# Two sequences' gate projections as twelve jobs of seven block products between retention and merge, in an encoder layer on one core

## The chip, the cores and the metric

The kernel runs on one core of a Trainium2 chip. The metric is the time of one execution on the device in microseconds; the number given for a kernel is the median of several executions.

## What is computed

One encoder layer is applied with the same weights to two batches: a prompt of 512 tokens and a sample of 1024 tokens, all in fp32. Cut to what bears on the change, and then the final norm:

```python
u = rms_norm(x, norm1_g)
proj = u @ w_in                       # 1024 -> 5632
f, q, k, v, g_ret, g_a, g_b = jnp.split(proj, list(np.cumsum(IN_SPLITS[:-1])), axis=-1)
branch_a = fourier_mix(f) @ w_four_proj                     # 512 -> 1024
branch_b = bidirectional_retention(q, k, v, g_ret, ret_decay_logit) @ w_ret_proj
merged = jax.nn.sigmoid(g_a) * branch_a + jax.nn.sigmoid(g_b) * branch_b
x = x + merged @ w_out
u2 = rms_norm(x, norm2_g)
h_gate, h_val = jnp.split(u2 @ w_up, 2, axis=-1)
# a convolution of width 3 and a GELU on h_gate, times h_val, then w_down and the residual
```

`bidirectional_retention` normalises its output per head and multiplies it with `jax.nn.silu(g_ret)`. The three gates g_ret, g_a and g_b are 1024 columns each.

## The kernel before, in words

**Layout.** Activations lie with the features on the partitions and the tokens along the free axis. The 1536 tokens are three blocks of 512 columns: t = 0 is the prompt, t = 1 and 2 are the two halves of the sample. A feature block is 128 rows, so 1024 features are eight blocks k. What does not fit on chip is spilled to DRAM in tiles of 128x512 (256 KB): `ma` for the Fourier branch, `sb` for the g_b gate, `og` for the retention output, each by feature block n and token block t.

**Products.** An fp32 product is made of three matmuls of a rounded type: every operand is split into a high part (a cast on ScalarE, ACT, L74) and the rest (a subtraction on VectorE, DVE, L75), and `mm3` (L110 to L112) adds high times high, high times low, low times high. A gate projection for one column block n and one token block t is therefore 8 x 3 = 24 matmuls of 512 columns. There are 3 gates x 8 blocks n x 3 blocks t = 72 of them.

**Stages.** Head: norms, the Fourier projection and the two DFTs. Then the stage called four projection here (a loop over n, L458 to L492): for each n a weight slab `wfour` (L461) is loaded, the Fourier branch `br` is computed in 258-column matmuls, and the three g_a gates of that n are projected, sent through a sigmoid (`gate`, L308 to L312), multiplied with `br` (L491) and stored as `ma` (L492). Then retention: four head pairs; `ret_main` projects q, k, v, hands each chunk of 128 tokens to a side generator, and projects the six g_ret gates of the pair as filling work; `ret_store` transposes the normalised output (L643), multiplies it with the gate (L644) and stores `og` (L645). `gb_main` projects the g_b gates: one column block in the DFT, four behind `ret_main` beside the last chunks, three around the start of the merge. Then the merge: `og` is loaded and split, multiplied with the slabs of `w_ret_proj` (`wslab`, L93), combined with `sb` and `ma` (loaded at L878 and L879), multiplied with `w_out`, added to x, and split. Then the up-projection and the down-projection.

**The up-projection's scheme.** For t = 1, 2 together, and by halves for t = 0, the up-projection is done as a 2x2 block product in seven block products in place of eight (`quad`). `w_ops` loads a raw weight block of 1 MB and forms four differences of it on DVE, splitting all; seven activation operands (A11, S1, S2, A12, S3, S4, A22, four row blocks each, high and low) lie on chip. One up job is 7 x 4 x 3 = 84 matmuls of 512 columns. `quads` runs jobs behind each other, with the elementwise work of a job one job late.

**What sets the order.** The program is written out in order, and each engine runs its own instructions in that order. SyncE (SP) issues the loads and nearly all stores in one queue of program order: a store that waits for its data holds up every load written behind it. Filling work is pulled one step at a time by generators. Buffers come from pools with a fixed number per tag.

Of the kernel before, what the change touches and what calls it, by code (L numbers as in the profile page):

```python
# [14 lines left out]
P = 128  # L15
# [9 lines left out]
SL_F, SL_GA, SL_GRET, SL_QKV, SL_GB = 0, 4, 12, 20, 36  # L25
SL_RP, SL_WO, SL_DL = 44, 52, 60
N_SLABS = 62
# [8 lines left out]
def emit(ctx, tc, x, wsl, wup, wdq, wd0, wfour, tab, cst, rcst, vec, out):  # L36
# [4 lines left out]
    uctx, wctx = ExitStack(), ExitStack()  # L41
    upool = uctx.enter_context(tc.tile_pool(name="u", bufs=24))
# [25 lines left out]
    x2_d = [[spill(f"xx{n}_{t}") for t in range(3)] for n in range(KD)]  # L68

    def utile(kind, dtype=F32R):  # L70
        return upool.tile([P, TC], dtype, name=kind, tag=kind)
# [5 lines left out]
    state = {"ww": (1152, 1032)}  # L77
# [5 lines left out]
    def wtiles():  # L83
        wpool = state["w"]
        wide, cols = state["ww"]
        r = wpool.tile([P, wide], F32, name="wr", tag="wr", bufs=2)
# [73 lines left out]
    state["w"] = wctx.enter_context(tc.tile_pool(name="w", bufs=4, reuse_waits="tile"))  # L160
    bctx = ExitStack()
    rc = bctx.enter_context(tc.tile_pool(name="rc", bufs=1, reuse_waits="tile"))
    state.update(wx=bctx.enter_context(tc.tile_pool(name="wx", bufs=1, reuse_waits="tile")), turn=-1)
# [10 lines left out]
    class Prep:  # L174
# [15 lines left out]
        def scale(self):  # L190
            k = len(u[self.t][0])
            xs = self.xs[k]
            g = vc[:, V_G1 + k:V_G1 + k + 1]
            h, l = utile("uh"), utile("ul")
# [12 lines left out]
        def rows(self):  # L207
            ps = rstd_rows(rcol[self.t])
            rrow[self.t] = rc.tile([P, TC], F32, name=f"rrow{self.t}")
# [98 lines left out]
    def gate(pool, tag, ps, t, bufs=None):  # L308
        sg = pool.tile([P, TC], F32, name="sg", tag=tag, bufs=bufs)
        nc.vector.tensor_tensor(sg, ps, rrow[t], op=ALU.mult)  # L310
# [3 lines left out]
    def gb_main(ns, pool, tag, bufs=None):  # L314
# [122 lines left out]

    z10 = channel_dft(1, 0)
# [7 lines left out]
    for q in preps:  # L446
        q.rows()
    z11 = channel_dft(1, 1)
    fill = gb_main(range(1), fp, "f2", 13)
# [7 lines left out]
    f2 = f2ctx.enter_context(tc.tile_pool(name="f2", bufs=2, side="right", reuse_waits="tile"))  # L457
    for n in range(KD):  # L458
# [55 lines left out]
    class Seq:  # L514
        def __init__(self, hp, si):
            self.hp, self.si = hp, si
            self.S, self.qd, self.os = {}, {}, {}
            self.st = None
# [82 lines left out]
    def ret_states(sq):  # L601
# [10 lines left out]
        for q in range(nt):  # L612
# [24 lines left out]
            yield  # L637

    def ret_store(sq, q, i, sg):
# [4 lines left out]
        nc.vector.tensor_tensor(sg, ps, sg, op=ALU.mult)  # L644
        nc.sync.dma_start(og_d[2 * sq.hp + i][t], sg)  # L645

    def ret_stores(todo):
        for args in todo:
            ret_store(*args)
            yield  # L650

    def ret_main():
        for hp in range(4):
# [18 lines left out]
            wg = [wslab(SL_GRET + 2 * hp + i) for i in range(2)]  # L672
            todo = []
            for t in range(3):
                for i in range(2):
                    ps = bank()
                    for _ in proj_steps(ps, wg[i], u[t]):
                        yield
                    g = rp.tile([P, TC], F32, name="g", tag="g")
                    sg = rp.tile([P, TC], F32, name="sg", tag="sg", bufs=4)  # L680
                    nc.vector.tensor_tensor(g, ps, rrow[t], op=ALU.mult)
                    nc.scalar.activation(sg, g, AF.Sigmoid)
                    nc.gpsimd.tensor_tensor(sg, g, sg, op=ALU.mult)
                    todo.append((seqs[0], 0, i, sg) if t == 0 else (seqs[1], t - 1, i, sg))
                    yield
                if t == 0 and hp < 3:
                    decay_t(hp + 1)
                if t == 0:
                    sides.append(ret_stores(todo))
                    todo = []  # L690
            sides.append(ret_stores(todo))

    decay_t(0)
    drive(ret_main())
    drive(gb_main(range(1, 5), rp, "g"))
# [4 lines left out]
    cp = cctx.enter_context(tc.tile_pool(name="mrg", bufs=5, side="right", reuse_waits="tile"))  # L700

    def og_split(t):
        gh, gl = [], []
        for k in range(KD):
            o = cp.tile([P, TC], F32, name="og", tag="st")
            l = cp.tile([P, TC], F32R, name="gl", tag="gl", bufs=KD)
            h = cp.tile([P, TC], F32R, name="gh", tag="gh", bufs=KD)
# [6 lines left out]
    drive(gb_main(range(5, 6), cp, "st"))  # L714
    order = (1, 2, 0)
    og = og_split(order[0])
    drive(gb_main(range(6, 8), cp, "st"))
    bctx.close()
    wctx.close()
    uctx.close()  # L720


    def left(name, bufs=1, stack=ctx):
        return stack.enter_context(tc.tile_pool(name=name, bufs=bufs, reuse_waits="tile"))

    def right(name, bufs, stack):
        return stack.enter_context(tc.tile_pool(name=name, bufs=bufs, side="right", reuse_waits="tile"))
# [5 lines left out]
    state["ww"] = 2048, 1024  # L733
    obctx, occtx = ExitStack(), ExitStack()
# [3 lines left out]
    xp = left("xs", 6, nctx)  # L738
# [45 lines left out]

    def chain(*gens):
        for g in gens:
            yield from g
            yield

    def w_ops(src, w):  # L790
        raw = wp.tile([P, 2048], F32, name="wr", tag="wr", bufs=2)[:, :4 * w]
        nc.sync.dma_start(raw, src)
        b = raw.rearrange("p (b c) -> p b c", b=4)

        def hl(src, n):
            tag, bufs = ("w", 4) if n == 2 else ("w4", 1)
            l = wp.tile([P, n * 512], F32R, name=tag + "l", tag=tag + "l", bufs=bufs)[:, :n * w]
            h = wp.tile([P, n * 512], F32R, name=tag + "h", tag=tag + "h", bufs=bufs)[:, :n * w]
            split(h, l, src)
            return [(h[:, i * w:(i + 1) * w], l[:, i * w:(i + 1) * w]) for i in range(n)]  # L800

        b11, b21 = hl(raw[:, :2 * w], 2)
        ta = wp.tile([P, 1024], F32, name="wt", tag="wt", bufs=2)[:, :2 * w]
        nc.vector.tensor_tensor(ta.rearrange("p (b c) -> p b c", b=2), b[:, 2:4], b[:, 0:3:2], op=ALU.subtract)
        t1, t3 = hl(ta, 2)
        tb = wp.tile([P, 1024], F32, name="wt", tag="wt", bufs=2)[:, :2 * w]
        nc.vector.tensor_tensor(tb[:, :w], b[:, 3], ta[:, :w], op=ALU.subtract)
        nc.vector.tensor_tensor(tb[:, w:], b[:, 1], tb[:, :w], op=ALU.subtract)
        t2, t4 = hl(tb, 2)
        b22, = hl(b[:, 3], 1)  # L810
        return {"A11": b11, "A12": b21, "S4": b22, "A22": t4, "S1": t1, "S2": t2, "S3": t3}

    def product(ps, w, act, name, start=False):
        n = len(act[name])
        for k, (h, l) in enumerate(act[name]):
            c = slice(k * P, (k + 1) * P)
            wh, wl = w[name]
            mm3(ps, wh[:, c], wl[:, c], h, l, start and k == 0, k == n - 1, not start)

    def quad(w, act, cols, sink):  # L820

        a = bank(cols)
        product(a, w, act, "A11", start=True)
        sink("P1", a)
        yield
        c = bank(cols)
        product(c, w, act, "S1", start=True)
        product(a, w, act, "S2")
        sink("P1+P6", a)
        b = bank(cols)  # L830
        product(b, w, act, "A12", start=True)
        sink("P2", b)
        product(a, w, act, "S3")
        sink("P1+P6+P7,P5", (a, c))
        yield
        product(c, w, act, "S4")
        sink("P5+P3", c)
        product(a, w, act, "A22")
        sink("P1+P6+P7+P4", a)
        yield  # L840

    late = []

    def tick():
        for it in list(late):
            if next(it, late) is late:
                late.remove(it)

# [476 lines left out]
```

## Time and profile before

| | |
|---|---|
| median of 3 runs | 2282.09 us (2281.72 to 2283.24) |
| the profiled execution | 2279.94 us, span 2277.8 us, granted clock 0.991 |
| TensorE (PE) matmuls busy | 2228.0 us, 98% |
| DVE busy | 1474.6 us, 65% |
| ACT busy | 848.5 us, 37% |
| GpSimd (POOL) busy | 345.8 us, 15% |
| DMA moved | 273.30 MB, mean 120 GB/s |

The stages in the trace: head up to about 165 us, four projection 165 to 340, retention 340 to about 830, the g_b tail to 971, merge from 975, then the up- and down-projection. A busy PE row means that a matmul was in flight; a PE clock of 1.00 in a window means that the throttle granted full speed in all of it.

### The profile page before, as it was taken

How to read it: one execution, taken by the hardware profiler on the slowest of the kernel's cores; microseconds unless marked ns; L12 is line 12 of the kernel's file. 1: busy time of each engine (PE TensorE's matmuls, PEld its weight loads, DVE VectorE, ACT ScalarE, POOL GpSimd, SP SyncE). 2: the span in 40 equal slices, each digit the busy share in tenths (PEclk: the TensorE clock that was granted, in tenths of full speed). 3: DMA queues.
4: the chain of work that ended last, by engine and by line, in shares of the span. 5: the costliest groups of instructions: out<-in, count | busy, mean ns of one | idle time of the engine just before them, and what ended most of it. 6: DMA issues, size and time to landing. Idle time of an engine off the chain costs nothing. (4 is left out here: it accounts for less than half of the span.)

```text
span 2277.8 us, 29367 instructions
## 1 busy us (share of the span) xinstructions
PE 2228.0 (98%) x11294; PEld 1866.6 (82%) x11294; DVE 1474.6 (65%) x2555; ACT 848.5 (37%) x1373; POOL 345.8 (15%) x184
## 2 busy tenths in 40 slices
PE   8899999999999999999999999999989999999997
PEld 6788888888888888878887788888867878999986
DVE  7453434656556462255678886767689888999744
ACT  6251222223121221133334444434453446666413
POOL 2799601111212120010120000000000000000001
PEclk9999999999999999999999999999999999999999
DMA  5252220111102012276756452323265455333462
GB/s 190 66 167 86 94 84 1 47 38 38 47 17 68 1 56 79 74 243 224 226 180 226 147 191 94 110 93 116 84 226 176 153 203 195 101 104 112 166 208 70
DMA packets 103531, 273.30 MB, mean 120 GB/s; under 512 B 11488, under 2 KB 14816, under 8 KB 97760
## 3 DMA queue, kind: packets, MB, share of 16 engines
q1 hardware_dynamic: 99936, 265.15, 35.1%
q10 hardware_dynamic: 3456, 6.29, 0.7%
q8 instruction: 88, 1.44, 0.3%
q14 instruction: 51, 0.42, 0.1%
HBM read 208.22 MB, written 63.18 MB: 119 GB/s over the span
## 5 line engine op out<-in xcount | busy, mean ns | idle before, releaser
L110 PE MATMUL bank<-op,wh 128*128 128x512 f32 (+1 forms) x1320 | 462.0, 352 | 8.0 <-DVE y L1096 4.2
L111 PE MATMUL bank<-op,wl 128*128 128x512 f32 (+1 forms) x1320 | 463.2, 351 | 1.1 <-DVE wl L75 1.1
L112 PE MATMUL bank<-op,wh 128*128 128x512 f32 (+1 forms) x1320 | 461.6, 350 | 1.1 <-DVE op L75 1.1
L75 DVE TENSOR_TENSOR wl<-wr,wh 128x1024 fp32r<-128x1024 f32 (+5 forms) x210 | 250.3, 1193 | 163.5 <-ACT wh L74 161.7
L74 ACT CAST wh<-wr 128x1024 fp32r<-128x1024 f32 (+5 forms) x210 | 204.8, 977 | 325.1 <-PE bank L112 220.7
L110 PEld LDWEIGHTS bank<-op,wh 128*128 128x128 f32 x1320 | 250.0, 189 | 48.3 <-DVE y L1096 5.2
L112 PEld LDWEIGHTS bank<-op,wh 128*128 128x128 f32 x1320 | 250.4, 190 | 37.6 <-DVE op L75 2.0
L111 PEld LDWEIGHTS bank<-op,wl 128*128 128x128 f32 x1320 | 250.3, 190 | 36.4 <-DVE wl L75 1.6
L110 PE MATMUL bank<-uh,wh 128*128 128x512 f32 x672 | 271.5, 404 | 5.2 <-ACT wh L74 5.2
L112 PE MATMUL bank<-ul,wh 128*128 128x512 f32 x672 | 266.0, 396 | 0.0
L111 PE MATMUL bank<-uh,wl 128*128 128x512 f32 x672 | 265.9, 396 | 0.0
L134 POOL TENSOR_TENSOR nr<-nv,mhalf 128x4 f32<-128x4 f32 (+1 forms) x10 | 12.9, 1285 | 1105.7 <-DVE nv L133 1075.8
L425 POOL TENSOR_TENSOR D<-two,D 128x64 f32<-128x64 f32 x16 | 170.2, 10667 | 0.0
L74 ACT CAST wh<-wt 128x1024 fp32r<-128x1024 f32 (+2 forms) x120 | 117.3, 977 | 135.9 <-PE bank L112 123.9
L110 PE MATMUL bank<-wh,uh 128*128 128x512 f32 x384 | 166.6, 434 | 0.0
L110 PEld LDWEIGHTS bank<-uh,wh 128*128 128x128 f32 x672 | 126.8, 189 | 32.1 <-ACT wh L74 5.2
L111 PE MATMUL bank<-wh,ul 128*128 128x512 f32 x384 | 151.4, 394 | 0.0
L112 PE MATMUL bank<-wl,uh 128*128 128x512 f32 x384 | 151.0, 393 | 0.0
L112 PEld LDWEIGHTS bank<-ul,wh 128*128 128x128 f32 x672 | 126.6, 188 | 29.4
L111 PEld LDWEIGHTS bank<-uh,wl 128*128 128x128 f32 x672 | 126.8, 189 | 27.7 <-DVE wl L75 0.8
L310 DVE TENSOR_TENSOR sg<-bank,rrow 128x512 f32<-128x512 f32 x48 | 33.2, 691 | 165.5 <-PE bank L112 165.5
L75 DVE TENSOR_TENSOR wl<-wt,wh 128x1024 fp32r<-128x1024 f32 (+2 forms) x120 | 135.6, 1130 | 6.5 <-ACT wh L74 6.3
(233 smaller groups left out, 4108.5 us busy)
## 6 DMA issues: line engine op xcount, KB each, us to landing
wr<-wsl SPq DMA_DIRECT2D x92, 512.0 KB, 3.9
wr<-wup SPq DMA_DIRECT2D x44, 1024.0 KB, 4.9
xs<-x SPq DMA_DIRECT2D x48, 256.0 KB, 4.2
wr<-tab SPq DMA_DIRECT2D x18, 516.0 KB, 3.7
wr<-wdq SPq DMA_DIRECT2D x12, 768.0 KB, 4.2
wr<-wd SPq DMA_DIRECT2D x16, 512.0 KB, 3.9
sb<-sg ACTq DMA_DIRECT2D x24, 256.0 KB, 2.0
ma<-sg SPq DMA_DIRECT2D x24, 256.0 KB, 2.0
```

What stands on the lines that cost most here:

```text
L74: nc.scalar.copy(h, src)
L75: nc.vector.tensor_tensor(l, src, h.bitcast(F32), op=ALU.subtract)
L110: nc.tensor.matmul(o, lh, rh, start=first, stop=False, skip_group_check=go_on)
L111: nc.tensor.matmul(o, ll, rh, start=False, stop=False, skip_group_check=go_on)
L112: nc.tensor.matmul(o, lh, rl, start=False, stop=last, skip_group_check=go_on)
L134: nc.gpsimd.tensor_tensor(r, v, mhalf[:, 0:n], op=ALU.pow)
L310: nc.vector.tensor_tensor(sg, ps, rrow[t], op=ALU.mult)
L425: nc.gpsimd.tensor_tensor(D[:, m], two.broadcast_to([P, 64]), D[:, m], op=ALU.pow)
```

## The change

For t = 1 and 2 the gates leave the places named above. For the prompt (t = 0) all 24 projections stay direct: `first_gates` for g_b (two blocks in the DFT, three behind `ret_main`, three before the new stage), `first_ret_gate` for g_ret (blocks 0 to 3 in the four projection loop, stored to DRAM and loaded again by the first two head pairs; 4 to 7 in `ret_main`), g_a in the loop as before.

The 48 projections of t = 1 and 2 become twelve jobs of `quad`, 84 matmuls each. A job takes a pair of column blocks: (g_b, g_a) of one n for i = 0 to 7, two g_ret blocks for i = 8 to 11. The jobs run between retention and merge, 8 to 11 first.

Their activation operands, 7 names x 4 row blocks x 2 parts = 56 tiles of 256 KB, are built by `u_ops(k)` in the four projection loop from x loaded again (16 loads), through two buffers `bh`, stored to DRAM, and loaded later: A12, S3, S4, A22 in the last head pair (`last_projected`) into the memory that the sample's u had, and A11, S1, S2 behind retention.

For t = 1, 2 `ma` first receives the bare branch `br`, and `og` the bare retention output; `done` of a job loads them, multiplies with the gate and stores them. The merge's tiles now share the 24 buffers of the pool that held A11, S1 and S2. The silu product of g_ret moves from POOL to DVE. The up-projection's sink becomes the shared `pair_sink` with the same work. The core of the diff (`quad`, `product`, `quads` and `w_ops` are moved up; `w_ops` takes its pools and its number of raw buffers from `state`):

```diff
+    def first_gates(ns):
         for n in ns:
-            wgb = wslab(SL_GB + n)
-            for t in range(3):
-                ps = bank()
-                for _ in proj_steps(ps, wgb, u[t]):
-                    yield
-                sg = gate(pool, tag, ps, t, bufs)
-                nc.scalar.dma_start(sb_d[n][t], sg)
+            w = slab(wg[n, :, 1024:2048])
+            ps = bank()
+            for _ in proj_steps(ps, w, u[0]):
                 yield
+            nc.scalar.dma_start(sb_d[n][0], gate(ps))
+            yield
...
+    def u_ops(k):
+        def get(t, kk):
+            v = bo.tile([P, TC], F32, name="bx", tag="bx", bufs=3)
+            nc.sync.dma_start(v, x[t, kk])
+            nc.vector.scalar_tensor_tensor(v, v, vc[:, V_G1 + kk:V_G1 + kk + 1], rrow[t], op0=ALU.mult, op1=ALU.mult)
+            return v
+        def put(name, src):
+            h, l = (bo.tile([P, TC], F32R, name="bh", tag="bh", bufs=2) for _ in range(2))
+            split(h, l, src)
+            for a, d in zip((h, l), uop_d[name][k]):
+                nc.sync.dma_start(d, a.bitcast(F32))
+        a21, s = get(2, k), get(2, k + 4)
+        put("A22", s)
+        yield
...
+    build = chain(*(u_ops(k) for k in range(4)))
+    fill = chain(*(first_ret_gate(n) for n in range(4)))
     for n in range(KD):
...
-        wga = wslab(SL_GA + n)
-        for t in range(3):
-            sg = gate(f2, "sga", proj(wga, u[t]), t)
-            nc.vector.tensor_tensor(sg, sg, br[:, t * TC:(t + 1) * TC], op=ALU.mult)
-            nc.sync.dma_start(ma_d[n][t], sg)
+        next(build, None)
+        next(build, None)
+        wga = slab(wg[n, :, 0:1024])
+        sg = gate(proj(wga, u[0]))
+        nc.vector.tensor_tensor(sg, sg, br[:, 0:TC], op=ALU.mult)
+        nc.sync.dma_start(ma_d[n][0], sg)
+        for t in (1, 2):
+            nc.sync.dma_start(ma_d[n][t], br[:, t * TC:(t + 1) * TC])
+        next(build, None)
+        next(build, None)
+        next(fill, None)
+        next(fill, None)
...
     drive(ret_main())
-    drive(gb_main(range(1, 5), rp, "g"))
+    drive(first_gates(range(2, 5)))
     while sides:
         drive([0])
     rctx.close()
...
+    ob = right("ob", 24, cctx)
+    for name in ("A11", "S1", "S2"):
+        load_op(ob, name)
...
+    def gate_job(i):
+        g, v, b = ([ut.tile([P, TC], F32, name="gv", tag="u") for _ in range(2)] for _ in range(3))
+        if i < 8:
+            jobs = ((v, None, sb_d[i]), (g, ma_d[i], ma_d[i]))
+        else:
+            jobs = ((g, og_d[2 * i - 16], og_d[2 * i - 16]), (v, og_d[2 * i - 15], og_d[2 * i - 15]))
+        def done():
+            for q, src, dst in jobs:
+                for a, c, t in zip(q, b, (1, 2)):
+                    if src:
+                        nc.sync.dma_start(c, src[t])
+                        nc.vector.tensor_tensor(c, c, a, op=ALU.mult) if i >= 8 else None
+                    nc.scalar.activation(a, a, AF.Sigmoid)
+                    if src:
+                        nc.vector.tensor_tensor(a, a, c, op=ALU.mult)
+                    nc.sync.dma_start(dst[t], a)
+        return lambda: w_ops(wg[i], 512), uop, TC, pair_sink(g, v), done
+    for _ in first_gates(range(5, 8)):
+        pass
+    for _ in quads(gate_job(i) for i in (*range(8, 12), *range(8))):
+        pass
```

Three places in the engines' order show what moved.

**First place: SP in the four projection loop.** Before, the rows from one `wfour` slab to the next, with `ma_0_83` the store of one column block's t = 0:

```order
L461 DMA wr<-wfour 128x1152
L492 DMA ma_2_82<-sg 128x512
L93 DMA wr<-wsl 128x1024
L492 DMA ma_0_83<-sg 128x512
L492 DMA ma_1_84<-sg 128x512
L461 DMA wr<-wfour 128x1152
```

After, the like stretch of the same queue, ahead of the next `wfour` slab; `A12h`, `S4l` and so on are the operand tiles, `bh` the buffers that they are built in, `bx` the loaded x:

```order
L604 DMA A12h_196<-bh 128x512
L665 DMA ma_0_83<-sg 128x512
L97 DMA wr<-wg 128x1024
L604 DMA A12l_197<-bh 128x512
L596 DMA bx<-x 128x512
L604 DMA S4h_212<-bh 128x512
L667 DMA ma_1_87<-br 128x512
L667 DMA ma_2_88<-br 128x512
L604 DMA S4l_213<-bh 128x512
L604 DMA A22h_222<-bh 128x512
L596 DMA bx<-x 128x512
L633 DMA wr<-wfour 128x1152
```

Between two weight loads now stand operand stores, each of which waits for its tile, and loads of x.

**Second place: the end of retention.** On PE before, the last transposes of retention (L643, of `o`, the normalised output) stand among g_b products:

```order
L112 MATMUL bank<-ul,wh 128x512
L643 MATMUL bank<-cs,o 128x128 x4
L110 MATMUL bank<-uh,wh 128x512
L111 MATMUL bank<-uh,wl 128x512
L112 MATMUL bank<-ul,wh 128x512
```

After, the last products of state and query (L804), the last transposes (L832) and then the g_b products of blocks 5 to 7 for t = 0:

```order
L115 MATMUL bank<-u,wl 128x512
L116 MATMUL bank<-u,wh 128x512
L804 MATMUL bank<-S,qd 128x128 x7
L832 MATMUL bank<-cs,o 128x128 x8
L114 MATMUL bank<-u,wh 128x512
```

Nothing stands between the L804 rows and the L832 rows now. On SP after, what follows the last retention stores (`s` is an operand tile on chip, `wr_7216` the raw weight of the first job):

```order
L838 DMA og_2_142<-sg 128x512
L838 DMA og_2_145<-sg 128x512
L890 DMA s<-A11h_170 128x512
L890 DMA s<-A11l_171 128x512
...
L890 DMA s<-S2h_192 128x512
L890 DMA s<-S2l_193 128x512
L172 DMA wr_7216<-wg 128x2048
L172 DMA wr_7313<-wg 128x2048
```

All 24 operand loads stand ahead of the first job's weight.

**Third place: SP at the start of the merge.** Before, the first slab of `w_ret_proj` (`wr<-wsl`) stands right behind the eight loads of `og` and ahead of the loads of `sb` and `ma`:

```order
L708 DMA og<-og_1_147 128x512
L93 DMA wr<-wsl 128x1024
L878 DMA sb<-sb_1_102 128x512
L879 DMA ma<-ma_1_78 128x512
L93 DMA wr<-wsl 128x1024
```

After, behind the loads of `og`, with `ma_1_96` and `ma_2_97` the products of the last job:

```order
L958 DMA og<-og_1_144 128x512
L929 DMA gv<-ma_1_96 128x512
L929 DMA gv<-ma_2_97 128x512
L1061 DMA xs<-x 128x512
L1039 DMA sb<-sb_1_99 128x512
L1040 DMA ma<-ma_1_75 128x512
L934 DMA ma_1_96<-gv 128x512
L934 DMA ma_2_97<-gv 128x512
L1039 DMA sb<-sb_1_102 128x512
L1040 DMA ma<-ma_1_78 128x512
L1039 DMA sb<-sb_1_105 128x512
L97 DMA wr<-wsl 128x1024 x2
```

The first slab moved behind the last job's two `ma` stores.

More of the change, by code (lines that the diff above doesn't have):

```diff
@@ L33, with emit @@
 V_G1, V_G2, V_GF, V_CW, V_CB, V_DL, V_END = 0, 8, 16, 24, 90, 112, 128
-def emit(ctx, tc, x, wsl, wup, wdq, wd0, wfour, tab, cst, rcst, vec, out):
+def emit(ctx, tc, x, wsl, wg, wup, wdq, wd0, wfour, tab, cst, rcst, vec, out):
     nc = tc.nc
@@ new lines, in product, with quad @@
+    def product(ps, w, act, name, start=False):
+        n = len(act[name])
+        for k, (h, l) in enumerate(act[name]):
+            c = slice(k * P, (k + 1) * P)
+            wh, wl = w[name]
+            mm3(ps, wh[:, c], wl[:, c], h, l, start and k == 0, k == n - 1, not start)
+    def quad(w, act, cols, sink):
+        a = bank(cols)
+        product(a, w, act, "A11", start=True)
+        sink("P1", a)
+        yield
+        c = bank(cols)
+        product(c, w, act, "S1", start=True)
+        product(a, w, act, "S2")
+        sink("P1+P6", a)
+        b = bank(cols)
+        product(b, w, act, "A12", start=True)
+        sink("P2", b)
+        product(a, w, act, "S3")
+        sink("P1+P6+P7,P5", (a, c))
+        yield
+        product(c, w, act, "S4")
+        sink("P5+P3", c)
+        product(a, w, act, "A22")
+        sink("P1+P6+P7+P4", a)
+        yield
@@ new lines, in emit, with tick, quads @@
+    late = []
+    def tick():
+        for it in list(late):
+            if next(it, late) is late:
+                late.remove(it)
+    def quads(jobs):
+        prev = None
+        for prep, act, cols, sink, after in jobs:
+            w = prep()
+            g = quad(w, act, cols, sink)
+            next(g)
+            if prev:
+                next(prev[0])
+                prev[1]()
+                tick()
+            next(g)
+            tick()
+            prev = g, after
+            yield
+        next(prev[0])
+        prev[1]()
+        tick()
@@ L165, in emit @@
+    bctx, ufctx, xctx = ExitStack(), ExitStack(), ExitStack()
+    rc = left("rc", 1, bctx)
+    ut = left("ut", 16, bctx)
+    state["w"] = left("w", 4, bctx)
+    uf = left("uf", 32, ufctx)
+    state.update(wx=left("wx", 1, xctx), turn=-1)
     fctx = ExitStack()
@@ L436, in decay_t @@
         nc.vector.tensor_copy(decT[hp], ps)
+    preps[0].rows()
+    state["gp"] = fp, "f2", 13
     z10 = channel_dft(1, 0)
@@ L445, in emit @@
     state["turn"] = -1
-    for q in preps:
-        q.rows()
     z11 = channel_dft(1, 1)
-    fill = gb_main(range(1), fp, "f2", 13)
+    fill = first_gates(range(2))
     next(fill)
@@ L671, in ret_main, with store, load_op, last_projected @@
                     yield
[L672 to L691, printed above, removed]
+            if hp == 3:
+                last_projected()
+            for i in range(2):
+                n = 2 * hp + i
+                def store(sg):
+                    assert seqs[0].ready
+                    sides.append(first_store(seqs[0], i, sg))
+                if hp < 2:
+                    sg = gtile("sg")
+                    nc.sync.dma_start(sg, og_d[n][0])
+                    store(sg)
+                else:
+                    yield from first_ret_gate(n, store)
+            if hp < 3:
+                decay_t(hp + 1)
+    uop = {}
+    def load_op(pool, name):
+        uop[name] = []
+        for k in range(4):
+            hl = [pool.tile([P, TC], F32R, name="s", tag="s") for _ in "hl"]
+            for o, d in zip(hl, uop_d[name][k]):
+                nc.sync.dma_start(o.bitcast(F32), d)
+            uop[name].append(hl)
+    goctx, gtctx = ExitStack(), ExitStack()
+    def last_projected():
+        state["wx"] = None
+        xctx.close()
+        ufctx.close()
+        oa = left("oa", 32, goctx)
+        for name in ("A12", "S3", "S4", "A22"):
+            load_op(oa, name)
     decay_t(0)
+    state["gp"] = rp, "sg", 4
     drive(ret_main())
-    drive(gb_main(range(1, 5), rp, "g"))
+    drive(first_gates(range(2, 5)))
     while sides:
@@ L783, in u_ops @@
         uop["S4"][k] = op_split(k, s4)
[L785 to L840, printed above, removed]
```

221 lines of the change are left out of this document (139 added, 82 removed).

## The prediction

> **What bounds the kernel now.** The first view is the page: busy time by engine, the chain that ended last, the DMA queues.
>
> ```profile
> PE 2228.0 (98%) x11294; PEld 1866.6 (82%) x11294; DVE 1474.6 (65%) x2555; ACT 848.5 (37%) x1373; POOL 345.8 (15%) x184
> q1 hardware_dynamic: 99936, 265.15, 35.1%
> PE 42%; DVE 2%; DMA 1%; ACT 1%; issue 1%; POOL 0%; SPq 0%; POOLq 0%; DVEq 0%; ACTq 0%
> ```
>
> PE has a matmul in flight in 2228.0 of 2277.8 us. Only 50 us are left in which it waits, so a removed matmul is time won, as long as nothing new makes PE wait. The second view, the windows, shows how near the others are, stage by stage. Columns are window, length, then busy time and instructions of PE, PE's weight loads, DVE, ACT and POOL, the granted clock, the DMA share and GB/s.
>
> ```profile
> 165.00:340.00 175.00, 175.00 (x903) 148.44 (x902) 74.67 (x134) 39.32 (x66) 98.21 (x13) 1.00 0.29 91
> 340.00:460.00 120.00, 119.38 (x614) 99.74 (x613) 67.14 (x205) 30.11 (x70) 19.76 (x23) 1.00 0.09 27
> 821.00:930.00 109.00, 108.95 (x503) 88.96 (x502) 38.29 (x98) 16.02 (x24) 10.86 (x8) 1.00 0.18 61
> 1350.00:1790.00 440.00, 430.93 (x1834) 344.94 (x1833) 329.88 (x415) 184.68 (x251) 0.00 (x0) 0.99 0.37 128
> ```
>
> The first row is the four projection, the second a head pair of retention, the third the g_b tail. In all three PE never waits, and DVE, ACT and DMA are far below it. The gates are that cover: long runs of matmuls which depend on little. The change takes just this work out of these places.
>
> **Term 1: the matmuls, −30.** The starts of the gate's first DVE operation show the pace of a direct projection, and those of the up job's last copy the pace of a block product job.
>
> ```profile
> 195.54 0.69 DVE L310 TENSOR_TENSOR sg<-bank,rrow 128x512 f32<-128x512 f32 x1 [2.65 <-PE bank L112]
> 201.04 0.69 DVE L310 TENSOR_TENSOR sg<-bank,rrow 128x512 f32<-128x512 f32 x1 [3.41 <-PE bank L112]
> 206.53 0.69 DVE L310 TENSOR_TENSOR sg<-bank,rrow 128x512 f32<-128x512 f32 x1 [3.42 <-PE bank L112]
> ...
> L954 ACT COPY g<-bank x7: 586/586/586, 1414.3 to 1531.6; 128x512 f32<-128x512 f32 x7
> ```
>
> A projection takes (206.53 − 195.54)/2 = 5.495 us, 0.229 a matmul. Seven copies span 117.3 us, six jobs: 19.55 us a job. 48 x 5.495 = 263.8 us go and 12 x 19.55 = 234.6 us come: −29.2. Counted by slots, 144 fewer matmuls x 0.229 = −33. I take −30, range −33 to −28.
>
> **Term 2: the four projection loop, +15.** 16 of its 24 g_a projections leave and 4 of g_ret come: PE falls from 175 to 175 − 12 x 5.495 = 109 us. Into the same stretch come 28 pairs of operand tiles. The rows that price them:
>
> ```profile
> L310 DVE TENSOR_TENSOR sg<-bank,rrow 128x512 f32<-128x512 f32 x48 | 33.2, 691 | 165.5 <-PE bank L112 165.5
> L767 DVE SCALAR_TENSOR_TENSOR xs<-xs,vc,rr 128x512 f32<-128x512 f32 x16 | 13.8, 879 | 6.4 <-DMA xs<-xx 6.4
> ...
> 1301.95 0.62 ACT L74 CAST hl<-xk 128x512 fp32r<-128x512 f32 x1 [2.56 <-issue]
> 1304.72 0.62 ACT L74 CAST hl<-xk 128x512 fp32r<-128x512 f32 x1 [1.19 <-DMA ox1h<-hl]
> ...
> ma<-sg SPq DMA_DIRECT2D x24, 256.0 KB, 2.0
> os34l<-hl SPq DMA_DIRECT2D x4, 256.0 KB, 5.3
> wr<-wup SPq DMA_DIRECT2D x44, 1024.0 KB, 4.9
> ```
>
> *DVE*: 74.7 us before; less 16 gates x 2 x 0.69 = 22; plus 28 splits and 16 differences x 0.69 = 30, 16 scalings x 0.88 = 14, the four g_ret gates' operations and slab splits and the moved norm rows, some 10: about 107 us. *DMA*: 56 stores, 16 loads of x, 24 `ma`, 4 `og` at 0.262 MB, 8 `wfour` slabs of 576 KB and 12 gate slabs of 512 KB make 37.2 MB. While busy the queue moved 265.15 MB in 35.1% of 2277.8 us = 332 GB/s, so 37.2 MB take 112 us. *The puts*: a put is cast, store, and the next cast on the same buffer. Before, the same pattern with two buffers (the rows of 1301.95 and 1304.72, the second released by the store) took 2.77 us: 28 of them 78 us; with a store landing in 5.3 us, the longest row of such a store, 28 x (0.62 + 5.3) = 166 us. Four resources between 78 and 166 us, coupled by in-order queues: stores that wait stand on SP ahead of the next `wfour` and gate slabs, and DVE's splits stand ahead of the operations that free PE's banks. The lower end is +0, all below PE's 109; the upper is 166 less the last four puts, which can run beside the head of retention (24), less 109: +33. I take DMA's 112 us, the row nearest to all four, plus some 12 us of coupling, an estimate of half a put for each block n (8 x 1.4 us, rounded up): 124, so +15.
>
> By the Trainium skill ("DMA: Bandwidth & Descriptors", Specifications) the limit of a core's HBM share is about 358 GB/s. No window of this trace reaches it; by it the 37.2 MB would take 104 us and this term would be +7.
>
> **Term 3: retention loses its fill, +3, and its last pair gets 32 loads, +2.** A head pair loses four g_ret projections, 22 of 120 us, and in the first two pairs all six. PE keeps 87 to 98 us against DVE's 67 − 6 = 61; the twelve chunks' chain has less work beside it. Lower end 0, since DVE keeps slack; upper 10, half of the 20 us by which POOL, DVE and ACT (19.8 + 67 + 30 in the second window) would exceed the rest if they ran one behind another. In the last pair 32 operand loads stand on SP ahead of a gate slab: 8.4 MB at 332 GB/s are 25 us, of which PE's fill covers most: 0 to 5, taken +2.
>
> **Term 4: the end of retention and the first job, +22.** After the last products of state and query, L832's transposes need the normalised output, and PE has nothing between (second place of the change).
>
> ```profile
> L622 DVE TENSOR_TENSOR o<-bank,o 128x256 f32<-128x256 f32 x48 | 20.3, 422 | 32.5 <-PE bank L621 32.1
> L624 DVE BATCH_NORM_STATS2 st<-o 128x6 f32<-128x128 f32 x96 | 23.2, 283 | 0.9
> L625 DVE BATCH_NORM_AGGREGATE mv<-st 128x2 f32<-128x6 f32 x96 | 14.9, 172 | 0.1
> L628 POOL TENSOR_TENSOR rr<-rr,mhalf 128x8 f32<-128x8 f32 x12 | 20.6, 1713 | 33.9 <-DVE rr L627 33.4
> L635 DVE TENSOR_SCALAR o<-o,mv,rr 128x128 f32<-128x128 f32 x96 | 27.2, 351 | 19.3 <-POOL rr L628 19.3
> L75 DVE TENSOR_TENSOR wl<-wr,wh 128x1024 fp32r<-128x1024 f32 x152 | 197.5, 1299 | 118.7 <-ACT wh L74 117.3
> L74 ACT CAST wh<-wr 128x1024 fp32r<-128x1024 f32 x152 | 159.6, 1050 | 242.6 <-PE bank L112 164.8 <-DMA wr<-wsl 24.5 <-issue 19.8
> ```
>
> For the last block: 0.42 + 8 x 0.283 + 8 x 0.172 + 1.71 + 8 x 0.351 = 8.6 us, 9 with the small L627. Before, g_b products covered it (108.95 of 109). Then three g_b projections, 16.5 us of PE. Behind the last `og` store SP issues 24 operand loads, 6.3 MB or 19 us, and only then the first job's weight, 1 MB: 3 us, some 2 to land, cast 1.05, split 1.30. The first product starts 26 us behind that store and PE has 18 us (the three projections and a slow start): a gap of 8, between 5 and 14.
>
> What an idle PE costs beside the gap, the trace shows twice:
>
> ```profile
> 65.11 1.02 PE L112 MATMUL bank<-wl,zh 128*128 128x258 f32 x3 [8.04 <-DVE wl L75]
> ...
> 974.79 0.65 PE L110 MATMUL bank<-gh,wh 128*128 128x512 f32 x1 [3.24 <-ACT wh L74]
> 977.07 0.63 PE L110 MATMUL bank<-gh,wh 128*128 128x512 f32 x1
> 977.49 0.63 PE L111 MATMUL bank<-gh,wl 128*128 128x512 f32 x1
> ```
>
> Behind 3.24 us of idling the pitch is 0.42 to 0.43 in place of 0.229. Either new gap (9 and 8 us) is longer, so each adds about 2.5 us of half pace: 9 + 2.5 + 8 + 2.7 = 22. Bounds: 12 (half of each covered) to 28.
>
> **Term 5: the merge's start, +8.** Before, the first slab was issued while g_b products still ran:
>
> ```profile
> 969.95 0.33 SPq L93 DMA_DIRECT2D wr<-wsl  x1
> 973.69 1.04 ACT L74 CAST wh<-wr 128x1024 fp32r<-128x1024 f32 x1 [0.75 <-DMA wr<-wsl]
> 974.77 1.23 DVE L75 TENSOR_TENSOR wl<-wr,wh 128x1024 fp32r<-128x1024 f32 x1 [2.49 <-ACT wh L74]
> ```
>
> PE waited 3.24 + 0.61 us. After, the slab stands behind the last job's `ma` stores (third place), which need the last product, a copy (0.59), four sigmoids (0.63 each), a DVE multiplication (0.69): 4 us; then some five issues (1.6), landing 3.7 (969.95 to 973.69), cast 1.05, with the DVE queue in between about 12. +8, from +5 to +11.
>
> **Term 6: the new stage itself, +2.** In the up-projection PE is busy 430.93 of 440 with DVE at 330, gelu and convolution included, work that the new jobs do not have. They have one raw weight buffer where the up-projection has two; with a load of 4.9 us within 19.55 us that is covered. 0 to +6. POOL's 24 products that go to DVE (0.69 each) hide in both places: 0. Operations moved to earlier in the head: 0 (±3).
>
> **Sum.** −30 + 15 + 3 + 2 + 22 + 8 + 2 = +22; 2279.94 + 22 = 2302 in the terms of the profiled execution, which lies 2.15 us below the median of 2282.09: **2304**.
>
> **Rivals.** *(a) The gaps are covered* and the saving stands: the puts run at 2.77 us and 332 GB/s is reached beside PE, so the loop stays bound by PE; the gaps of terms 4 and 5 are half as wide. −30 + 0 + 1 + 14 + 4 = −11: 2271; with every term at its lower end −33 + 0 + 0 + 12 + 5 = −16: 2266; with no gap at all 2250. For it: in the loop PE, DVE and DMA differ by a few us. It decides if the loop takes under 112 us and the operand loads are issued before the last `og` store is through. Against: the order of SP leaves no such room. *(b) The loop is paced by the puts* at the landing of the loaded rows (5.3): +33 in place of +15: 2322, and with PE's waits in it over 3.2 us each, eight half-paced starts of 2 us: 2338. The Trainium skill ("TensorE: Matmul & The Clock Gate", The HAM clock gate) has this rule: after an idle window of about 3.4 us the array runs at half clock until it was busy for as long. The rows behind 974.79 agree. By it the loop pays only if its waits come in one piece. *(c) The products don't shrink as counted*: jobs at 22 us (the 0.229 pace x 84 is 19.2, so nothing speaks for it) would cost 29 more: 2333.
>
> **How the numbers follow.** Forecast with its own range 2288 to 2320: 0.45. (a) 0.33, of which 0.07 within 0.2% of before. (b) 0.17. (c) 0.02. Between forecast and (a), 0.03 within 0.2%. 0.2% (4.6 us) is about what a measurement of this kernel can tell from no change. Faster 0.26, same 0.10, slower 0.64. The range reaches to 2258, into (a) short of its far end, and to 2336.
>
> **What would show it.** Right: the four projection stage some 125 us long with PE idle behind DVE or DMA; a gap of 9 us ahead of the last transposes, one of 8 us ahead of the first block product released by the weight's cast; one of about 12 at the merge's start; half-paced matmuls behind each; jobs of 19.5 us. Wrong: a loop of 110 us with PE full, or operand loads landed before the last g_b projection ends, would bring (a); a loop of over 145 us (b).

## The result and the profile after

The changed kernel takes 2318.45 us (median of 4, 2317.77 to 2320.89) against 2281.9 us of the kernel before, measured beside it: a ratio of 1.0165, 95% interval 1.0148 to 1.0183. It is slower by 37 us.

The page of the changed kernel, as the one of before was read: busy time of the engines, and the DMA queue.

```profile
PE 2213.2 (96%) x11150; PEld 1849.8 (80%) x11150; DVE 1587.4 (69%) x2711; ACT 942.6 (41%) x1513; POOL 313.8 (14%) x160
q1 hardware_dynamic: 132192, 333.32, 42.8%
```

144 matmuls are gone, yet PE's busy time fell only from 2228.0 to 2213.2 us, and its idle time rose from 49.8 to 2316.0 − 2213.2 = 102.8 us. The windows of the changed kernel show in which stages (length, then busy time of PE, weight loads, DVE, ACT, POOL; granted clock, DMA share, GB/s):

```profile
0.00:158.00 158.00, 142.68 (x800) 120.67 (x801) 92.83 (x184) 77.09 (x129) 105.52 (x39) 0.97 0.46 144
158.00:270.00 112.00, 106.51 (x592) 91.57 (x591) 89.39 (x164) 45.86 (x80) 105.65 (x10) 0.98 0.86 289
270.00:300.00 30.00, 18.38 (x59) 12.81 (x60) 16.97 (x28) 8.61 (x13) 2.23 (x5) 0.77 0.67 223
300.00:700.00 400.00, 391.07 (x2081) 327.81 (x2080) 246.79 (x791) 111.37 (x269) 52.95 (x71) 1.00 0.15 52
700.00:764.00 64.00, 42.55 (x177) 33.56 (x176) 23.75 (x66) 12.43 (x17) 3.27 (x2) 0.82 0.61 215
764.00:998.00 234.00, 234.00 (x1004) 189.35 (x1002) 131.78 (x169) 100.66 (x146) 0.00 (x0) 0.99 0.41 142
998.00:1016.00 18.00, 3.27 (x8) 2.02 (x7) 4.52 (x6) 3.92 (x5) 0.00 (x0) 0.65 0.90 301
```

The rows are: head, the four projection loop, its end and the head of retention, retention, its end up to the first block product job, the twelve jobs, the start of the merge. In the jobs PE never waits. It waits at every seam around them: 17.1 us in the second and third row, 8.9 in retention, 21.5 ahead of the jobs, 14.7 behind them. The single waits, from PE's timeline (start, length, instruction, and in brackets the wait and what ended it):

```profile
294.11 0.90 PE L739 MATMUL bank<-cs,r 128*128 128x128 f32 x3 [8.16 <-DVE r L730]
711.89 0.50 PE L114 MATMUL bank<-u,wh 128*128 128x512 f32 x1 [2.88 <-ACT wh L78]
728.05 2.27 PE L832 MATMUL bank<-cs,o 128*128 128x128 f32 x8 [6.08 <-DVE o L818]
760.63 0.80 PE L114 MATMUL bank<-s,wh 128*128 128x512 f32 x1 [11.97 <-ACT wh L78]
1012.62 0.80 PE L114 MATMUL bank<-gh,wh 128*128 128x512 f32 x1 [14.26 <-ACT wh L78]
```

They are the first chunk of retention, a prompt gate whose slab stands behind the 32 operand loads, the last transposes, the first job's weight, and the merge's first slab. What DVE and ACT waited for shows where the first and the fourth come from. The first operation of the first chunk waits until the store of the last operand tile has landed. The first job's weight is issued by SP at 751.89 and cast at 759.53:

```profile
292.43 0.42 DVE L719 TENSOR_TENSOR t<-pr,rs 128x256 f32<-128x256 f32 x1 [2.67 <-DMA S4l<-bh]
751.89 13.35 SPq L172 DMA_DIRECT2D wr<-wg  x2
759.53 1.04 ACT L78 CAST wh<-wr 128x1024 fp32r<-128x1024 f32 x1 [9.48 <-DMA wr<-wg]
```

**The account.** What PE lost by running at a reduced clock is its busy time times (1 − granted clock), summed over windows of 2 us: 10.7 us before, 25.1 us after. So the span's 38.2 us are 53.0 us more of idling, 14.4 us more of reduced clock, and 29.2 us of matmul time saved, which is what remains. By place, after less before, idling and reduced clock together, beside the prediction's terms:

| place | idle | reduced clock | sum | predicted |
|---|---|---|---|---|
| head | −2.7 | −0.1 | −2.8 | 0 |
| four projection loop and head of retention | 17.1 | 5.9 | 23.0 | 15 |
| retention, 300 to 700 us | 6.2 | 0 | 6.2 | 5 |
| end of retention and first job | 21.5 | 7.8 | 29.3 | 22 |
| the jobs | 0 | 0 | 0 | 2 |
| start of the merge | 10.9 | −1.1 | 9.8 | 8 |
| behind it | 0 | 1.9 | 1.9 | 0 |
| matmuls saved | | | −29.2 | −30 |
| sum | | | 38.2 | 22 |

### The profile page after: what moved, and what is told of

Read it like the earlier page. It is cut to its first block, busy times and chain, and to the rows that moved or that the text cites. A ratio compares the mean times of both kernels' runs of the same rounds, so it can differ in the third digit from the quotient of the medians.

```text
span 2316.0 us, 29681 instructions
## 1 busy us (share of the span) xinstructions
PE 2213.2 (96%) x11150; PEld 1849.8 (80%) x11150; DVE 1587.4 (69%) x2711; ACT 942.6 (41%) x1513; POOL 313.8 (14%) x160
## 5 line engine op out<-in xcount | busy, mean ns | idle before, releaser
L79 DVE TENSOR_TENSOR wl<-wr,wh 128x1024 fp32r<-128x1024 f32 (+5 forms) x222 | 267.0, 1205 | 181.3 <-ACT wh L78 179.7
L78 ACT CAST wh<-wt 128x1024 fp32r<-128x1024 f32 (+2 forms) x144 | 142.4, 989 | 168.7 <-PE bank L116 148.1
L79 DVE TENSOR_TENSOR wl<-wt,wh 128x1024 fp32r<-128x1024 f32 (+2 forms) x144 | 165.1, 1146 | 10.7 <-ACT wh L78 10.3
L114 PE MATMUL bank<-wh,u 128*128 128x512 f32 x384 | 168.4, 439 | 2.0 <-ACT wh L78 2.0
L116 PE MATMUL bank<-wl,u 128*128 128x512 f32 x384 | 152.4, 397 | 2.2 <-DVE wl L79 2.1
L115 PE MATMUL bank<-wh,u 128*128 128x512 f32 x384 | 152.5, 397 | 0.0
L184 DVE TENSOR_TENSOR wt<-wr 128x1024 f32<-128x1024 f32 (+2 forms) x72 | 82.4, 1145 | 68.0 <-DMA wr<-wg 66.7
L114 PE MATMUL bank<-u,wh 128*128 128x512 f32 x288 | 118.8, 412 | 10.3 <-ACT wh L78 8.1
L114 PE MATMUL bank<-s,wh 128*128 128x512 f32 x288 | 114.8, 398 | 12.0 <-ACT wh L78 12.0
L116 PE MATMUL bank<-u,wh 128*128 128x512 f32 x288 | 116.4, 404 | 4.3 <-DVE u L306 4.3
L115 PE MATMUL bank<-u,wl 128*128 128x512 f32 x288 | 116.7, 405 | 0.0
L115 PE MATMUL bank<-s,wl 128*128 128x512 f32 x288 | 114.9, 399 | 0.5 <-DVE wl L79 0.5
L116 PE MATMUL bank<-s,wh 128*128 128x512 f32 x288 | 114.9, 399 | 0.0
```

What stands on the lines that cost most here:

```text
L78: nc.scalar.copy(h, src)
L79: nc.vector.tensor_tensor(l, src, h.bitcast(F32), op=ALU.subtract)
L114: nc.tensor.matmul(o, lh, rh, start=first, stop=False, skip_group_check=go_on)
L115: nc.tensor.matmul(o, ll, rh, start=False, stop=False, skip_group_check=go_on)
L116: nc.tensor.matmul(o, lh, rl, start=False, stop=last, skip_group_check=go_on)
```

## The experiments

Times are medians, each beside the kernel before on the same chip (2280.9 to 2282.3 us in these runs).

### The first job's weight ahead of the operands

```diff
+    gt = left("gt", 2, gtctx)
+    state["raw"] = gt.tile([P, 2048], F32, name="wr2", tag="wr2", bufs=1)
+    nc.sync.dma_start(state["raw"], wg[8])
     ob = right("ob", 24, cctx)
     for name in ("A11", "S1", "S2"):
         load_op(ob, name)
```

> Against the changed kernel's 2318.4. Theory (issue order): PE waited 11.97 us ahead of the first block product because its 1 MB weight is issued behind 24 operand loads; with the weight issued first the gap closes to under 2 us and the half pace behind it goes: 2303 to 2307. Rival (bytes): the same 7.3 MB must land before the job can run, so the wait only moves to the operands: 2314 to 2319.

Measured: 2304.32 us (2302.3 to 2305.93), ratio to before 1.0100 (1.0083 to 1.0117): 14.1 us less than the changed kernel. In its timeline no wait is left ahead of the first job, and two short ones stand a little way into it:

```profile
762.61 0.51 PE L116 MATMUL bank<-s,wh 128*128 128x512 f32 x1 [1.59 <-DMA s<-S2l]
763.79 0.50 PE L114 MATMUL bank<-s,wh 128*128 128x512 f32 x1 [0.67 <-ACT gv L257]
```

The theory of the issue order holds. The operands do arrive just in time (1.59 us on the last S2 tile), the weight was late only by its place in the queue.

### Three merge slabs during the last job

```diff
-    for _ in quads(gate_job(i) for i in (*range(8, 12), *range(8))):
-        pass
+    first_rp = []
+    for i, _ in enumerate(quads(gate_job(i) for i in (*range(8, 12), *range(8)))):
+        if i == 11:
+            first_rp += [wslab(SL_RP + n) for n in range(3)]
...
-            w = wslab(SL_RP + n)
+            w = first_rp.pop(0) if first_rp else wslab(SL_RP + n)
```

> The first three slabs of the merge are loaded and split during the last block product job, in buffers that are idle there. Theory (slab late): the 14.26 us that PE waits at the start of the merge are the slab's issue behind the last job's stores, its landing and its split; gone, with 2 us of half pace: 2303 to 2307. Rival (elementwise chain): the merge's first product also needs the last split of the retention output, 1001.5 against the last block product's end at 998.4; then the gap falls only to 3 to 4 us, and if the sb and ma tiles are late as well to 8: 2308 to 2312.

Measured: 2315.95 us (2310.42 to 2318.18), ratio 1.0150 (1.0135 to 1.0165): 2.5 us less, where both theories expected more. The interval overlaps that of the changed kernel, so even these 2.5 us are not clear of noise. The products of the merge do begin at once: this row of their tile's view gives the first and the last start of the merge's first-operand matmuls, in the changed kernel and then here.

```profile
L114 PE MATMUL bank<-gh,wh x192: 392/392/795, 1012.6 to 1239.6; 128*128 128x512 f32 x192
```

```profile
L114 PE MATMUL bank<-gh,wh x192: 388/392/795, 998.3 to 1232.6; 128*128 128x512 f32 x192
```

The two waits of this run's timeline that tell where the time went again:

```profile
1021.06 0.80 PE L114 MATMUL bank<-gh,wh 128*128 128x512 f32 x1 [5.95 <-ACT wh L78]
1287.29 0.80 PE L116 MATMUL bank<-op,wh 128*128 128x512 f32 x1 [2.98 <-DVE op L79]
```

14.3 us are won at the first product and 7.0 are left at the last. The wait moved to the fourth slab (5.95 us, with half pace behind it). At the start of the up-projection PE then waits 2.98 us for DVE's split of an operand, where the changed kernel waits 0.66. From the end of the merge to there (1233 to 1314 us, against 1240 to 1320 in the changed kernel) idling is 2.2 us more and reduced clock 3.1. In the profiles 0.9 us are left at the end. The slab was one of two things that were late: behind it PE waits for DVE.

### Three buffers for the operand tiles

The edit is `bufs=3` in place of 2 for the tag `bh`.

> Three buffers for the operand tiles in place of two. Theory (buffer wait): the 28 pairs took 126 us, 4.5 us each, because a cast waits for the store two tiles back to land; with three the chain ends 15 to 25 us earlier, before the loop does, and PE's wait of 8.16 us at the head of retention and the half pace behind it go: 2304 to 2310. Rival (DMA rate): the loop moves some 290 GB/s at 0.87 of the DMA's time, so the chain ends at most 5 us earlier: 2314 to 2319.

Measured: 2320.23 us (2313.28 to 2321.73), ratio 1.0167 (1.0150 to 1.0183): no change. First the changed kernel's casts into these tiles (first and last start), then this run's:

```profile
L78 ACT CAST bh<-bx x28: 603/621/625, 162.9 to 287.8; 128x512 fp32r<-128x512 f32 x28
```

```profile
L78 ACT CAST bh<-bx x28: 602/621/628, 166.1 to 276.6; 128x512 fp32r<-128x512 f32 x28
```

The largest waits of its timeline in the loop:

```profile
198.50 0.78 PE L115 MATMUL bank<-u,wl 128*128 128x512 f32 x1 [2.15 <-DVE wl L79]
224.90 0.50 PE L115 MATMUL bank<-u,wl 128*128 128x512 f32 x1 [2.01 <-DVE wl L79]
259.44 0.79 PE L115 MATMUL bank<-u,wl 128*128 128x512 f32 x1 [2.90 <-DVE wl L79]
```

And one of its windows, in the columns of the windows above:

```profile
170.00:185.00 15.00, 15.00 (x85) 12.99 (x85) 13.16 (x24) 5.66 (x12) 15.00 (x2) 1.00 0.99 347
```

Either theory was half right. The chain ends 11 us earlier and the 8.16 us at the head of retention are gone. But the waits return inside the loop, on the weight slabs' splits: between 158 and 300 us 13.3 of the 17.1 us of idling are still there, and between 700 and 764 us PE idles 2.8 us more than in the changed kernel. The loop itself has no room. In its first part DMA is busy 0.99 of the time at 347 GB/s.

### The last three prompt gates beside the last chunks

```diff
-    drive(first_gates(range(2, 5)))
+    drive(first_gates(range(2, 8)))
...
-    for _ in first_gates(range(5, 8)):
-        pass
```

> The last three prompt gates run beside the last chunks of retention, no longer behind them. Theory: the 6.08 us ahead of the last transposes are covered, but the first block product is set by the last retention store plus loads and weight, so its gap grows from 12 to about 20 us and the sum stays: 2316 to 2320. Rival (covered wait is won): 2309 to 2312.

Measured: 2320.90 us (2319.45 to 2326.78), ratio 1.0180 (1.0165 to 1.0196): no gain. The wait ahead of the transposes is gone and the one ahead of the first job has doubled:

```profile
762.40 0.79 PE L114 MATMUL bank<-s,wh 128*128 128x512 f32 x1 [25.54 <-ACT wh L78]
```

The theory holds, though its 20 us were 25.54. The first job starts at 762.4 against 760.6: it is set by the last retention store, the loads and the weight, and cover that is moved ahead of these wins nothing.

### The operand tiles built during retention

The scaled rows of t = 1 and 2, `build` and the pool `bo` move from the loop to the start of retention; one step of `build` is taken per chunk. The spare weight buffers (`wx`) are closed there to make room.

```diff
-        next(build, None)
-        next(build, None)
         wga = slab(wg[n, :, 0:1024])
...
+    bo = right("bo", 1, rctx)
+    for t in (1, 2):
+        preps[t].rows()
+    build = chain(*(u_ops(k) for k in range(4)))
...
                     sides.append(ret_chunk(sq, c, ps))
+                    next(build, None)
                     yield
```

> The operand tiles are built and stored during the first head pairs of retention, no longer in the four projection loop. Against the changed kernel's 2318.4. Theory (the build is in the wrong place): PE's 9.1 us of waits in the loop, 9.0 us at the head of retention and some 5 us of half pace behind them go, and retention, where DMA moved 27 GB/s and DVE was busy 67 of 120 us, takes the build in its slack: 2296 to 2302. Rival (DVE order): in retention the splits stand ahead of the chunks' DVE operations, whose cover left with the gates, and PE waits there instead: 2312 to 2320.

Measured: 2303.18 us (2301.76 to 2306.67), ratio 1.0093 (1.0078 to 1.0109): 15.3 us less, 1 us above the theory's range. In its timeline PE has no wait of 0.4 us or more between 157 and 320 us. In retention the waits grew, the two largest of the first head pair and the largest of all being

```profile
320.73 0.70 PE L746 MATMUL bank<-qbd,kT 128*128 128x256 f32 x2 [1.70 <-DVE qbd L741]
385.49 0.70 PE L746 MATMUL bank<-qbd,kT 128*128 128x256 f32 x2 [1.45 <-DVE qbd L741]
558.65 0.70 PE L746 MATMUL bank<-qbd,kT 128*128 128x256 f32 x2 [2.30 <-DVE qbd L741]
```

The first chunk's transposes start 22.9 us earlier than in the changed kernel (271.2 for 294.1), the last chunk's 17.8 us earlier (668.1 for 685.9): retention gives 5 us back, so the rival came in part. For the most part the price of the build lay in its place, a loop that its own weights, stores and loads fill already.

### The retention gate direct again

`first_ret_gate` is called for all three t in `ret_main`, from one slab per block; jobs 8 to 11 are left out, and the first job's weight is issued first. The scaled rows of t = 1 and 2 stay in memory until the last head pair, and its 32 operand loads move behind its gates.

> The retention gate of t = 1 and 2 is projected directly in retention again, as before; the other eight jobs stay, and the first job's weight is issued first. Against the run with the weight first, 2304.3. Theory (missing cover): the waits of 10.9 us ahead of the score products in retention fall to about 2 as before the change, while 16 projections cost 16 x 5.495 - 4 x 19.55 = 9.7 us more than four jobs: 2302 to 2307. Rival (the waits belong to retention's own chain): they stay, and the projections come on top: 2311 to 2315.

Measured: 2307.74 us (2306.89 to 2311.39), ratio 1.0119 (1.0105 to 1.0132): 3.4 us more than with the weight first, between the ranges of the theory and the rival; the two intervals overlap, so the run shows no gain rather than a loss. All PE waits of 0.4 us or more between 300 and 817 us:

```profile
417.26 0.70 PE L753 MATMUL bank<-qbd,kT 128*128 128x256 f32 x2 [1.37 <-DVE qbd L748]
536.97 0.70 PE L753 MATMUL bank<-qbd,kT 128*128 128x256 f32 x2 [1.33 <-DVE qbd L748]
628.30 0.49 PE L807 MATMUL bank<-S,qd 128*128 128x128 f32 x2 [0.44 <-DVE S L794]
743.73 0.70 PE L753 MATMUL bank<-qbd,kT 128*128 128x256 f32 x2 [0.92 <-DVE qbd L748]
759.00 0.49 PE L807 MATMUL bank<-S,qd 128*128 128x128 f32 x2 [0.44 <-DVE S L794]
```

The wait ahead of the last transposes is not among them. The five waits add up to 4.5 us. In the run with the weight first, those of 0.4 us or more in retention (300 to 712 us) add up to 8.2, and in the kernel before (340 to 821 us) to 1.0. So the cover that left is a part of their cause; where the rest comes from stays open. The projections cost at least what the waits cost.

### All moved, twice

The first run joins four of these edits (build in retention, weight first, three slabs early, the gates beside the last chunks) and exchanges operands: A11, S1, S4, A22 are loaded in the last head pair, S2, A12, S3 behind retention.

> The build in retention, the first job's weight first, S2, A12 and S3 as the late operands, the last three prompt gates beside the last chunks, three merge slabs during the last job. Theory (gaps are separate): 2318.4 - 14 (weight) - 18 (build) - 8 (transposes) - 2.5 (slabs) = 2276, 2270 to 2282, at or under the kernel before (2281). Rival (given back): the start of the up-projection is bound by DVE and takes 5 to 8 us more of it, as with the early slabs: 2282 to 2290.

Measured: 2283.49 us (2279.71 to 2288.0), ratio 1.0011 (1.0002 to 1.0019). 35 us are won, 7 less than the sum of the terms. The time lies in the rival's range, but its cause hardly shows: from the end of the merge into the up-projection (1210 to 1285 us) idling and reduced clock are 1.8 us more than in the changed kernel (1240 to 1320 us), not 5 to 8. Three waits are left at the seams of the jobs:

```profile
729.88 0.79 PE L114 MATMUL bank<-s,wh 128*128 128x512 f32 x1 [6.03 <-ACT wh L78]
979.99 0.50 PE L114 MATMUL bank<-gh,wh 128*128 128x512 f32 x1 [1.96 <-ACT gh L78]
995.68 0.80 PE L114 MATMUL bank<-gh,wh 128*128 128x512 f32 x1 [6.93 <-ACT wh L78]
```

The second run puts one prompt gate beside the last chunks and two behind the transposes, and loads four slabs early.

> As the run with all moved, but one of the three last prompt gates beside the last chunks and two behind the last transposes, and four merge slabs during the last job. Against that run's 2283.5. Theory (cover goes where the wait is): its 6.03 us ahead of the first job fall to under 1, its 6.93 us at the merge's fourth slab go, with some 4 us of half pace, less 3 given back at the start of the up-projection: 2268 to 2275, under the kernel before by 0.3 to 0.6%. Rival (the bytes come due later): the operands of the first job land no earlier, so its wait moves behind its second product: 2278 to 2284.

Measured: 2281.85 us (2275.41 to 2285.23), ratio 0.9995 (0.9985 to 1.0006): the time of the kernel before, and again the rival's range. Its first job has no wait ahead of it, but two of 0.85 and 0.76 us inside; the transposes wait again and the merge's wait moved to its fifth slab:

```profile
716.13 0.70 PE L830 MATMUL bank<-cs,o 128*128 128x128 f32 x2 [3.81 <-DVE o L816]
994.48 0.80 PE L114 MATMUL bank<-gh,wh 128*128 128x512 f32 x1 [4.95 <-ACT wh L78]
1254.60 0.79 PE L116 MATMUL bank<-op,wh 128*128 128x512 f32 x1 [2.10 <-DVE op L79]
```

By the account from above, this run saves 31.1 us of matmul time against the kernel before and pays 23.3 us more of idling and 9.8 us more of reduced clock. The largest part lies in none of the seams but in retention: idle time and reduced clock there are 16.7 us more than in the kernel before. The windows of retention, in the kernel before and then here:

```profile
340.00:821.00 481.00, 478.35 (x2452) 398.76 (x2451) 270.29 (x808) 120.85 (x279) 82.03 (x92) 1.00 0.11 36
270.00:695.00 425.00, 407.24 (x2143) 339.01 (x2141) 290.19 (x875) 129.41 (x301) 62.21 (x74) 1.00 0.29 97
```

PE idles 17.8 us where it idled 2.7. Retention has lost its gates and taken in the build. No version here beats the kernel before.

## Why the prediction was right, and where its sizes were off

The direction and the mechanism hold: the matmuls are saved, and the seams that lost their cover together pay more than that. 2304 was forecast and 2318 measured, near the upper end of the range. Point by point:

- **Term 1** (−30): right, −29.2 by the account. The jobs run at 84 matmuls in 19.2 us once warm, not 19.55: their last copies run from 787.0 to 998.4 us, eleven jobs. By that pace the saving would be 33 us; the 4 us between the two stay open.
- **Term 2** (+15): the size was 23.0, and the place was another. The 124 us that were forecast for the loop are what the chain of puts took, 124.9 from the first cast to the last; with a third buffer it takes 110.5, near the 112 of DMA alone. But the step "coupling" expected PE to wait in the loop. There PE waits 5.5 us; 11.6 us more fall at its end and on the first chunk of retention, whose DVE operations stand behind the last splits of the build and wait for its last store. The overlap of the last four puts with retention, which the prediction had taken only as a discount on its upper end, was the place of the loss. The run with three buffers shows that one can hardly be had without the other: shorten the chain and PE waits in the loop. The build in retention shows what another place is worth: 15.3 us net.
- **Term 3** (+5): 6.2 us in retention, and 2.88 us on the prompt gate behind the 32 loads, which the table has in the row of the end of retention. The direct retention gate shows the missing cover as a part of the cause.
- **Term 4** (+22): right in both gaps, with other sizes: 6.08 for 9 ahead of the transposes, 11.97 for 8 ahead of the first job, as the weight took 7.6 us from issue to its cast, not 5. Moving the weight won 14.1 us. The mis-sized part is the half pace: 7.8 us for 5.2, since the 2.88 us wait has it too.
- **Term 5** (+8): 9.8 us, right. That the wait could be bought off was not claimed, and the early slabs show that it can hardly be: of the 14.3 us won at the first product 2.5 are left, within the noise.
- **Term 6** (+2): 0. The head, taken as 0, is 2.8 us faster: PE's 8.04 us wait at 65 us became 2.85, while one of 2.49 us at 49 us left and one of 4.27 at 41 came.
- **Reduced clock**: the step that was off most. It was priced at two gaps, 5.2 us; it is 14.4 in all. The row that it was priced by had cost more, too: behind 974.79 the reduced clock took 3.1 us (975 to 990), not the 2.5 to 2.7 priced.

Rival (a), covered gaps, did not come; rival (b), a loop paced by the puts, came in part, with a pace of 4.6 us a put (124.9 us from the first cast to the last, 27 steps) between the two that were priced.

One reading of the prediction is wrong, beside term 2: that no window of the trace before reaches 358 GB/s. Windows of 10 us moved 376 GB/s (from 1860 us) and 380 GB/s (from 2150 us), so this figure is no limit here. The sum did not use it.

## What to carry to other kernels

Work that is always ready is worth more than its own time where it stands between stages: before a product is made cheaper by a scheme with operands to build and load, list what each removed block covered, and price every seam, with the half pace behind it. Put the build where DMA and DVE have room, not where it is handy in the code, and issue the one transfer that the first instruction needs ahead of those that later ones need. A saving of 29 us in the busiest engine was here worth nothing even after most of the seams had been mended, as half of what still offsets it is lost in retention, which gave up its fill and took in the build.

## What had not been expected of the hardware

A wait of 2.17 us was once enough to halve PE's pace, and not at once. The changed kernel's timeline around such a wait:

```profile
216.78 0.47 PE L114 MATMUL bank<-u,wh 128*128 128x512 f32 x1 [2.17 <-DVE sg L424]
217.09 0.39 PE L115 MATMUL bank<-u,wl 128*128 128x512 f32 x1
...
218.26 0.63 PE L114 MATMUL bank<-u,wh 128*128 128x512 f32 x1
...
221.66 0.39 PE L116 MATMUL bank<-u,wh 128*128 128x512 f32 x1
```

For 1.5 us behind the wait the matmuls start 0.23 to 0.31 us apart, then for 3.4 us (218.26 to 221.66) 0.43 us apart, then 0.23 again. The prediction had taken 3.24 us, the shortest wait that it showed, as the mark. The Trainium skill ("TensorE: Matmul & The Clock Gate", The HAM clock gate) asks for at least one idle window of some 3.4 us; the 3.4 us of half pace agree with its window, the 2.17 us of idling do not. The half pace cost some 1.7 us here, half of 3.4, on top of the wait.

Not every such wait is followed by half pace. In the kernel before, the granted clock stays at 1.00 behind a wait of 2.62 us:

```profile
1211.72 0.50 PE L110 MATMUL bank<-mh,wh 128*128 128x512 f32 x1 [2.62 <-ACT mh L74]
1212.00:1222.00 10.00, 9.64 (x42) 7.64 (x42) 6.81 (x10) 4.50 (x7) 0.00 (x0) 1.00 0.63 209
```

In the changed kernel it is 0.57 from 1249 to 1253 us, behind a wait of 1.48 us at 1247.50. So the length of a wait alone does not decide it between 1.5 and 2.9 us: one of 2.89 us at 710.70, in the run with the gates beside the last chunks, has full pace behind it as well. What does decide it no run here shows.
